# A relative-position bias table in DRAM: written by one copy from DRAM one layer earlier, not from eight partitions inside the layer that reads it

## The chip, the core and the metric

The program runs on one NeuronCore of one Trainium2 chip. Its engines have separate instruction streams: PE (TensorE, matrix products), DVE (VectorE), ACT (ScalarE), POOL (GpSimd) and SP (SyncE, which here only issues DMAs). DMAs are issued by SP or by ACT, each on a queue of its own; the profile calls SP's q1 and ACT's q10. The metric is the device time of one execution in microseconds (us), lower is better.

## The reference

The reference runs two transformer-like blocks on 512 tokens of 1024 features, in float32. The second block has an even layer (retention and gated recurrence), an odd layer, and after each of them cross-attention with a memory and a convolved feed-forward. The change concerns the odd layer's mixer, an attention with eight heads of 128. To each score it adds a bias that depends on the distance of query and key alone. Three dilated branches are merged; in the kernel they are one causal attention, in which a key counts as often as branches hold its distance:

```
logits = q.k * hd**-0.5 + rel_bias[bucket(distance)] (by head)
weight of a key = number of branches that hold its distance (none: left out)
o = softmax(logits, counted by branch) @ v, by head; x = x + o @ w_out
```

So all that a head needs as a bias is one row of 640 numbers, one for each distance. For a tile of 128 queries by up to 512 keys, each query reads this row one place further on than the query before it.

## The kernel before

Activations stay on the chip, feature-major, as eight tiles of 128 features by 512 tokens. Float32 products are made of three products each: activations and weights are split in a high and a low part (`whi`, `wlo` for weights), and `proj` (lines 487, 490 and 491) multiplies high by high, low by high and high by low. Weights come in groups of 1 MB. `fetch` (L461) issues the load on SP's queue into `wraw`, which has two buffers; `wload` cuts it into pieces of 128x512, ACT casts a piece to `whi` (L474) and POOL makes `wlo` (L383). `whi` and `wlo` have four buffers each, and a piece feeds twelve products on PE.

The ten layer parts run in the order m0, f0, m1, f1, ev, xa0, g0, od, xa1, g1. Here g0 is the feed-forward part before the odd mixer od. In g0, `up_pair` makes two of 22 tiles: projections to `psb` and `ps`, DVE's `pad` and `cv`, ACT's L600 and L603, and the split of the result to `mid` (ACT's cast at L496).

In od, `_odd` first makes the bias. Table `tb` (33x640, constant) and `relb` (33x8) come by SP's queue, two products on PE give `ps` (8x640), DVE copies it to `fb` on 8 partitions, one partition to a head, and a DMA on SP's queue writes each head's row 128 times to DRAM, at a step of 641 numbers, as `biasscr`. Read back at a step of 640, row q of the table is thus shifted by q. `head` reads 256 KB of it as `bias` (three buffers) with one DMA for each head, and DVE adds it to the scores where it takes them out of PSUM (L1570). For eight heads, `qkv` of the next head is projected beside `head` of the present one; `ps` of the scores (L1568) has two buffers.

The program is written in Tile: it gives dependences, and a scheduler with a timing model puts each engine's instructions in order. An engine runs its stream in that order; a DMA that waits holds up what stands behind it in its issuer's stream. All DMAs take one of eight completion semaphores in turn, and a DMA waits until the one before it on its semaphore has landed.

Of the kernel before, what the change touches and what calls it, by code (L numbers as in the profile page):

```python
# [11 lines left out]
F32 = mybir.dt.float32  # L12
# [8 lines left out]
P = 128  # L21
# [3 lines left out]
EPS = 1e-6  # L25
# [5 lines left out]
# ---------------------------------------------------------------- host layout  # L31
def _perm_attn():
    """Columns of a pair of 64-wide heads: first rope halves of both, then second halves."""
    idx = []
    for half in range(2):
        for h in range(2):
            for ax in range(2):
                idx += [h * 64 + ax * 32 + half * 16 + f for f in range(16)]
    return np.array(idx)
# [5 lines left out]
def _pack_cols(w, kc, cg):  # L45
    """[L, kc*128, G*cg] -> [L, G, 128, kc*cg]: one contiguous run per partition."""
    w = np.asarray(w)
    L, K, N = w.shape
    g = N // cg
    a = w.reshape(L, kc, P, g, cg).transpose(0, 3, 2, 1, 4)  # L50
    return np.ascontiguousarray(a).reshape(L, g, P, kc * cg)


def _cols(v):
    """[..., n*128] -> [128, n] of the flattened vector."""
    return np.asarray(v).reshape(-1, P).T
# [5 lines left out]
def _vec_layout(inputs=None):  # L62
    """All per-feature vectors as columns of one [128, n] array; fills VEC with the places."""
# [12 lines left out]
    for l in range(DEPTH):  # L76
        add(f"nm{l}", 8, lambda: _cols(g("norm_mix_g")[l]))
        add(f"nf{l}", 8, lambda: _cols(g("norm_ffn_g")[l]))
        # conv taps: column = tile*5 + tap
# [3 lines left out]
        # (dir, pair) columns, the head of the pair by partition half  # L83
# [26 lines left out]
def _const_layout():  # L110
    """Constants of the shapes alone, [128, n] float32."""
# [57 lines left out]
# the heads of the even mixer in turn: 0 for a recurrent one, 1 for a retention one  # L169
EV_HEADS = ((1, 0), (0, 0), (1, 1), (0, 1), (1, 2), (0, 2), (0, 3), (1, 3))  # L170
RET_CDECAY = [float((1.0 - 2.0 ** (-5.0 - h)) ** P) for h in range(4)]
# columns of the retention table
# [4 lines left out]
def _hg_masks():  # L177
    """Causal pairs (key, query) of a block of 8; for blocks of 16 and 32, keys of the lower halves
    with the queries of the upper halves, which stand side by side."""
# [11 lines left out]
def _dsa_tables():  # L191
    """Rows 0-31: one-hot of the bucket of a distance; row 32: log of the number of branches that
    hold the distance, -1e30 where none does. Column m stands for distance 512 - m."""
# [12 lines left out]
def host_arrays(inputs):  # L206
# [15 lines left out]
    # z, and the rows of its product's projection: heads 0 2, 1 3, 4 6, 5 7 side by side  # L222
# [14 lines left out]
    # tiles of 128: the forget gates; by head in turn, its columns; outputs by head in turn  # L237
# [4 lines left out]
    # by head: q, k, v columns side by side  # L242
# [9 lines left out]
# steps of the fillers of the first block's mixer to one of what they stand beside: the work inside the  # L252
# chunks, the inverse, the scan, the attention; the parts of the first gates beside the first
# two; the second gates left for the ends of the scan and of the attention
# [5 lines left out]
# ---------------------------------------------------------------- the program  # L260
class Norm:
    """RMS norm of the feature-major residual: chunks x*g split in two float32r parts; the
    reciprocal root of each token, on all partitions, is applied where products leave PSUM."""
# [8 lines left out]
    def chunk(self, m):  # L272
# [12 lines left out]
        # the sums of the last chunk apart, the others' are done by then  # L285
# [7 lines left out]
        if self.n == 8:  # L293
            k.tok_sums(self.sums[:, 1], sq)
            k.tt(self.sums[:, 0], self.sums[:, 0], self.sums[:, 1], ALU.add)
            # the roots by token, their squares
# [9 lines left out]
class Prog:  # L306
    def __init__(self, ctx, tc, A, out, first):
# [19 lines left out]
        # the first weights amid the residual  # L327
# [12 lines left out]
    def banks(self, *bufs):  # L340
        """The PSUM banks besides those of the projections, in up to three rings."""
# [10 lines left out]
    @contextmanager  # L352
    def phase(self, name):
        """The pool of a layer part: temporaries by role."""
        with self.tc.tile_pool(name=f"ph_{name}", bufs=1) as self.ph:
            yield self.ph

    def gs(self, name, bufs=2, shape=(P, S), dt=F32):
        """A temporary of a role: its buffers go round in program order."""
# [25 lines left out]
    def rsqrt(self, out, in_, scale, eps):  # L385
        """out = (in_ * scale + eps) ** -0.5: a first guess from the exponent, Newton steps to
        float32's accuracy."""
# [12 lines left out]
    def issue_behind(self, ins, before):  # L400
        """Issue order on an engine, no wait."""
# [3 lines left out]
    # ---- head norms: reciprocal roots by tokens, then spread over the partitions  # L405
    def tok_sums(self, out, sq, view=None, nt=4, psum=None):
        """Of a feature-major tile: the sums by token over all features, or those that view(by token)
        ends with, [128 tok, nt, ...]."""
# [9 lines left out]
    def rs_cols(self, groups, view, ncol, scale, eps, nt=4, psum=None, r=None):  # L418
        """For each group, a feature-major tile of squares: the sums by token over the features that
        view(by token) ends with, [128 tok, nt, ncol] ** -0.5; with the norm r, of products  # L420
        that its root has not been applied to yet, times that root."""
# [20 lines left out]
    def spread(self, rc, wide=None, nt=4, psum=None):  # L442
        """PSUM [128, nt*128]: per token its column of rc on all partitions; wide(e, rc) lays the
        columns out over the partitions where there are several."""
# [13 lines left out]
    # ---- weights  # L458
# [5 lines left out]
    def wload(self, src, kc, cg, rows=False):  # L464
        """One group of weight columns: a list of 128 columns each, as pieces (first row tile, its
        two float32r parts [128, 4, 128]); or the pieces [128, 2, 256] of all its columns."""
# [13 lines left out]
    def proj(self, ps, w, acts, n=S, behind=None):  # L480
        """ps := the product; behind: the instruction to issue it behind."""
# [11 lines left out]
    def split(self, dst, src, eng="vector"):  # L493
        """dst [128, 2, n] float32r := the two parts of src (SBUF or, on the vector engine, PSUM)."""
# [14 lines left out]
    def silu2(self, x, out, t):  # L509
        """out = 2 silu(x), t a scratch tile"""  # L510
# [4 lines left out]
    def to_tok(self, src, o, n=4, eng="scalar", scale=None, ps=None):  # L515
        """o [128 tok, n, 128] of a feature-major tile."""
# [12 lines left out]
    # ---- out projection onto the residual  # L529
# [27 lines left out]
    # ---- feed-forward layers  # L557
    def ffn(self, l, second, nm, nxt):
# [3 lines left out]
        with self.phase("ffn") as fp, self.banks(2, 2):  # L562
# [62 lines left out]
            for mp in range(5):  # L625
                up_pair(mp)
            down(0)
# [7 lines left out]
    # ---- first block: attention beside the delta net  # L635
# [4 lines left out]
    def _mix(self, l, nm, nxt, mp):  # L640
# [4 lines left out]
        # by direction, pair, chunk: the keys with their decays; by head of the pair, what makes the outputs,  # L645
        # the queries with their decays in the head's rows, the products in the other's
# [5 lines left out]
        # inverses by direction and pair of chunks  # L652
# [32 lines left out]
        # -- q, k, v of the delta net: projection, convolution, silu  # L685
# [12 lines left out]
        kq = []                             # by pair: keys, queries  # L698
# [10 lines left out]
        # -- l2 norms of q and k  # L709
# [4 lines left out]
        def l2(pairs):  # L714
# [6 lines left out]
            # x comes doubled; the queries times dk ** -0.5  # L721
# [6 lines left out]
        # -- beta and decay, by (head of the pair, token of the chunk)  # L728
# [26 lines left out]
        # log(1 + e) = log(u) + (e - (u - 1)) / u for the rounded u = 1 + e  # L755
# [37 lines left out]
        def by_chunk(dst, src, ps, scale):  # L793
            """dst (head of the pair, token of the chunk), by chunks, of a feature-major pair"""
# [7 lines left out]
        # -- v, by token  # L802
# [11 lines left out]
        # -- inside the chunks: decays, products of keys and queries  # L814
# [49 lines left out]
        # -- the fillers: attention, its projection and gate  # L864
# [6 lines left out]
        def gained(w, gname):  # L871
            """The products of a tile of two heads times the gain, their squares; the root of the norm
            is still to be applied."""
# [13 lines left out]
        def qkv():  # L887
            """Keys of a group in both halves of the rows of each rope half, in two parts; values in
            two parts."""
# [19 lines left out]
        def queries(g):  # L909
            """By head, the second part where the other head of its tile stood; the scores take the  # L910
            roots, by token."""
# [97 lines left out]
        # -- inverse of the unit triangles, one to a partition  # L1009
        def solve(sp):  # L1010
# [5 lines left out]
            # the halves of the diagonal first  # L1016
# [9 lines left out]
            # for their joining: the first half's transpose in the free corner, forwards; both halves  # L1026
            # transposed, the second itself in the corner, backwards
# [16 lines left out]
        def merge(*gens):  # L1044
            """In turn."""
# [9 lines left out]
        class Side:  # L1055
            """A generator whose steps are spread over those of others."""
# [52 lines left out]
        # -- the scan over the chunks, both directions  # L1109
# [4 lines left out]
        # what is wanted of two chunks at a time: columns by head of the pair, the other's rows 0  # L1114
# [18 lines left out]
        # pairs of chunks in turn of the directions  # L1133
        pair = lambda u: (u % 2, u // 2 if u % 2 == 0 else 3 - u // 2)

        def load(u):
            """Keys and queries of two chunks."""
# [8 lines left out]
        def join(u):  # L1146
            """The inverses of two chunks from their halves."""
# [11 lines left out]
            # the chunks side by side in the array  # L1159
# [18 lines left out]
        def scan_step(n):  # L1178
# [8 lines left out]
            def times(w, x):  # L1187
                """By pair the block's columns of each head times x."""
# [6 lines left out]
            # by head its state in its rows, the new values in the other's  # L1195
# [60 lines left out]
        # -- norm of the outputs, gated by z, feature-major again  # L1256
# [12 lines left out]
        # half of the root: z comes as 2 silu(z)  # L1269
# [4 lines left out]
        # by tiles of two heads of the same place in their pairs  # L1274
# [28 lines left out]
    # ---- even mixer: retention heads and gated recurrent heads  # L1303
# [4 lines left out]
    def _even(self, nm, nxt, ep):  # L1308
# [10 lines left out]
        # lower bounds of the forget gates: softmax over the rows, its first row  # L1319
# [12 lines left out]
        # f = lb + (1 - lb) (1 + tanh(x / 2)) / 2 = fa tanh(x / 2) + fb  # L1332
# [449 lines left out]
```

## Time and profile before

| | |
|---|---|
| median of 3 runs | 3497.29 us (3495.54 to 3500.16) |
| profiled execution, span from its first to its last instruction | 3496.1 us |
| PE busy | 3232.1 us, 92% |
| DVE, ACT, POOL busy | 58%, 42%, 52% |
| DMA traffic | 342.51 MB, on average 98 GB/s |

The page gives the profiled execution by its span alone; the median of the runs is 1.2 us above that. PE is busy nearly throughout, so that a stretch in which it stands still is to be looked for. An engine's idle time is put down to what ended it: "PE ps L1568 <- DVE pr L1570" is PE at the products of line 1568, waiting for a DVE instruction of line 1570 that writes `pr`. Times within the execution count from the span's start.

### The profile page before, as it was taken

The numbers are of one execution on the slowest core, as the hardware profiler recorded it, in microseconds if no ns is written. First come the engines' busy times: TensorE is split into PE (matmuls) and PEld (weight loads), VectorE is DVE, ScalarE is ACT, GpSimd is POOL, SyncE is SP. The second block draws the span as 40 slices with busy tenths as digits, with TensorE's granted clock in tenths as the row PEclk, the third lists the DMA queues.
The fourth block names the chain that finished last, engine by engine and source line by source line (L and its number), as shares of the span: only waits on it lengthen the run. The fifth ranks groups of instructions, "written<-read, shape, count | busy, mean of one in ns | idle before, by whom it ended". The sixth has DMA issues, their size and how long they took to land. (4 is left out here: it accounts for less than half of the span.)

```text
span 3496.1 us, 46894 instructions
## 1 busy us (share of the span) xinstructions
PE 3232.1 (92%) x17342; PEld 2661.3 (76%) x17342; DVE 2028.2 (58%) x3571; ACT 1483.6 (42%) x2766; POOL 1806.7 (52%) x1493
## 2 busy tenths in 40 slices
PE   8878899999978889999999888999997799899999
PEld 6666778888766677888878777888885687878887
DVE  8988556463698855555466676552323586663222
ACT  4536434343553553434353335443433355544332
POOL 4653365444565335554456556465554235556554
PEclk9999999999999999999999999999998899999999
DMA  4532532222353244222222113222223312222222
GB/s 142 161 88 61 132 122 86 100 94 94 122 159 102 72 113 128 87 97 97 94 101 86 59 62 109 73 97 97 97 91 91 84 61 103 91 90 89 95 98 93
DMA packets 135844, 342.51 MB, mean 98 GB/s; under 512 B 43039, under 2 KB 80287, under 8 KB 106944
## 3 DMA queue, kind: packets, MB, share of 16 engines
q1 hardware_dynamic: 135328, 338.75, 30.5%
q8 instruction: 138, 2.26, 0.3%
q14 instruction: 90, 0.74, 0.1%
q10 hardware_dynamic: 288, 0.76, 0.1%
HBM read 309.53 MB, written 29.95 MB: 97 GB/s over the span
## 5 line engine op out<-in xcount | busy, mean ns | idle before, releaser
L383 POOL TENSOR_TENSOR wlo<-wraw,whi 128x512 fp32r<-128x512 f32 (+2 forms) x1044 | 1370.2, 1316 | 1449.5 <-ACT whi L474 1402.0
L474 ACT CAST whi<-wraw 128x512 fp32r<-128x512 f32 (+2 forms) x1044 | 631.4, 608 | 1134.3 <-PE psb L490 838.4
L487 PE MATMUL psb<-act,whi 128*128 128x512 f32 x1888 | 760.6, 403 | 60.3 <-DVE x L383 19.8
L491 PE MATMUL psb<-act,wlo 128*128 128x512 f32 x1888 | 752.7, 399 | 3.5 <-POOL wlo L383 3.4
L490 PE MATMUL psb<-act,whi 128*128 128x512 f32 x1888 | 755.0, 400 | 0.6 <-DVE act L277 0.6
L487 PEld LDWEIGHTS psb<-act,whi 128*128 128x128 f32 x1888 | 364.5, 193 | 140.8 <-issue 43.0
L491 PEld LDWEIGHTS psb<-act,wlo 128*128 128x128 f32 x1888 | 363.4, 192 | 81.6 <-POOL wlo L383 5.8
L490 PEld LDWEIGHTS psb<-act,whi 128*128 128x128 f32 x1888 | 364.3, 193 | 74.2 <-DVE act L277 1.9
L383 DVE TENSOR_TENSOR x<-psb,x 128x512 f32<-128x512 f32 x168 | 115.2, 689 | 378.1 <-PE psb L491 377.5
L487 PE MATMUL ps<-act,whi 128*128 128x512 f32 (+1 forms) x720 | 281.6, 391 | 3.4 <-ACT rB L303 3.4
L491 PE MATMUL ps<-act,wlo 128*128 128x512 f32 (+1 forms) x720 | 281.0, 390 | 0.0
L490 PE MATMUL ps<-act,whi 128*128 128x512 f32 (+1 forms) x720 | 281.0, 390 | 0.0
L487 PE MATMUL psb<-mid,whi 128*128 128x512 f32 x704 | 277.0, 394 | 1.0 <-DVE x L383 1.0
L491 PE MATMUL psb<-mid,wlo 128*128 128x512 f32 x704 | 276.2, 392 | 0.0
L490 PE MATMUL psb<-mid,whi 128*128 128x512 f32 x704 | 274.1, 389 | 0.0
L487 PEld LDWEIGHTS ps<-act,whi 128*128 128x128 f32 (+1 forms) x720 | 134.1, 186 | 33.8 <-ACT rB L303 4.6
L491 PEld LDWEIGHTS ps<-act,wlo 128*128 128x128 f32 (+1 forms) x720 | 134.1, 186 | 29.8 <-issue 0.8
L490 PEld LDWEIGHTS ps<-act,whi 128*128 128x128 f32 (+1 forms) x720 | 134.2, 186 | 29.3 <-issue 0.5
L491 PEld LDWEIGHTS psb<-mid,wlo 128*128 128x128 f32 x704 | 132.3, 188 | 30.3
L487 PEld LDWEIGHTS psb<-mid,whi 128*128 128x128 f32 x704 | 132.6, 188 | 29.4 <-DVE x L383 1.5
L490 PEld LDWEIGHTS psb<-mid,whi 128*128 128x128 f32 x704 | 132.3, 188 | 29.1
L383 DVE TENSOR_TENSOR cv<-ps,cv 128x512 f32<-128x512 f32 (+1 forms) x60 | 41.5, 692 | 175.8 <-PE ps L491 106.1
(437 smaller groups left out, 5712.8 us busy)
## 6 DMA issues: line engine op xcount, KB each, us to landing
wraw<-in_wup SPq DMA_DIRECT2D x44, 1024.0 KB, 4.8
wraw<-in_fup SPq DMA_DIRECT2D x44, 1024.0 KB, 4.8
wraw<-in_win SPq DMA_DIRECT2D x38, 1024.0 KB, 5.0
wraw<-in_wdn SPq DMA_DIRECT2D x16, 1024.0 KB, 4.8
wraw<-in_evin SPq DMA_DIRECT2D x16, 1024.0 KB, 4.8
wraw<-in_xakv SPq DMA_DIRECT2D x16, 1024.0 KB, 4.8
wraw<-in_fdn SPq DMA_DIRECT2D x16, 1024.0 KB, 4.9
wraw<-in_odin SPq DMA_DIRECT2D x12, 1024.0 KB, 4.8
```

What stands on the lines that cost most here:

```text
L383: getattr(self.nc, eng).tensor_tensor(out, a, b, op)
L474: nc.scalar.copy(hi, part)
L487: mm = nc.tensor.matmul(ps, hi[:, i], acts[k][:, 0, :n], start=k == 0, stop=False)
L490: nc.tensor.matmul(ps, hi[:, i], acts[k][:, 1, :n], start=False, stop=False)
L491: nc.tensor.matmul(ps, lo[:, i], acts[k][:, 0, :n], start=False, stop=k == kc - 1)
```

## The change

The making of the table moves out of `_odd` into a function `bias_rows`, which g0's `ffn` calls after its third `up_pair`, in the layer before the odd mixer. Its four DMAs are issued by ACT on ACT's queue. `fb` is first written to DRAM as `biasrow` (8 rows of 2560 bytes), and then one DMA from DRAM to DRAM copies these 128 times to `biasscr`. In this DMA the 128 copies are the outermost dimension, and the heads the next; before, the heads were the outermost. `tb`, `relb` and `fb` now lie in g0's pool. `_odd` only reads the finished table. The diff's other lines take out comments and docstrings, so that line numbers shift (L1560 to L1568, L1568 to L1576, L1570 to L1578).

```diff
@@ ffn @@
             for mp in range(5):
                 up_pair(mp)
+                if mp == 2 and l == 0 and second:
+                    self.bias_rows(fp)
             down(0)
...
+    def bias_rows(self, op):
+        nc = self.nc
+        tb, rb = op.tile([33, 640], F32, name="tb"), op.tile([33, 8], F32, name="relb")
+        nc.scalar.dma_start(out=tb, in_=self.A["dsat"])
+        nc.scalar.dma_start(out=rb, in_=self.A["relb"])
+        fb = op.tile([8, 640], F32, name="fb")
+        for a, b in ((0, 512), (512, 640)):
+            ps = self.pss()
+            nc.tensor.matmul(ps[:8, :b - a], rb, tb[:, a:b], start=True, stop=True)
+            nc.vector.tensor_copy(fb[:, a:b], ps[:8, :b - a])
+        row = self.dr.tile([8, 640], F32, name="biasrow")
+        nc.scalar.dma_start(out=row, in_=fb)
+        self.biasscr = self.dr.tile([8, P * 641], F32, name="biasscr")
+        nc.scalar.dma_start(out=self.biasscr.rearrange("h (q m) -> q h m", m=641)[:, :, :640],
+                            in_=row.unsqueeze(0).broadcast_to((P, 8, 640)))
...
     def _odd(self, nm, nxt, op):
         nc, gs = self.nc, self.gs
         win = self.A["odin"][0]
-        tb = op.tile([33, 640], F32, name="tb", tag="pT", bufs=2)
-        nc.sync.dma_start(out=tb, in_=self.A["dsat"])
-        rb = op.tile([33, 8], F32, name="relb")
-        nc.sync.dma_start(out=rb, in_=self.A["relb"])
-        scr = self.dr.tile([8, P * 641], F32, name="biasscr")
-        fb = op.tile([8, 640], F32, name="fb", tag="pT", bufs=2)
...
-        nc.sync.dma_start(out=scr.rearrange("h (q m) -> h q m", m=641)[:, :, :640], in_=fb.unsqueeze(1).broadcast_to((8, P, 640)))
+        scr = self.biasscr
```

Three places show how the scheduler's order moves. The first is SP's queue at the beginning of the odd mixer; `wraw<-in_odin` are the mixer's weight loads. Before:

```order
L461 DMA wraw<-in_odin 128x2048 x2
L1511 DMA tb<-in_dsat 33x640
L1513 DMA relb<-in_relb 33x8
L461 DMA wraw<-in_odin 128x2048 x2
L1521 DMA biasscr<-fb 1024x1x640
L461 DMA wraw<-in_odin 128x2048
L1560 DMA bias<-biasscr 128x512 x3
L461 DMA wraw<-in_odin 128x2048
```

The same place of the changed kernel:

```order
L461 DMA wraw<-in_odin 128x2048 x2
L1568 DMA bias<-biasscr 128x512 x3
L461 DMA wraw<-in_odin 128x2048 x4
L1568 DMA bias<-biasscr 128x512
L461 DMA wraw<-in_odin 128x2048
```

The write of the table is gone from this queue, and the first three heads' reads of it stand two weight loads after the mixer's first, where `tb` and `relb` stood.

The second place is ACT in g0, after the sixth tile's `mid`; DMAHW4_49 and the like are the semaphores that a row waits for. Changed kernel only (before, the rows are the same without the two DMAs):

```order
L496 CAST mid<-cv 128x512 [waits DVE_49]
L1516 DMA biasrow<-fb 8x640 [waits DMAHW4_49,DVE_49]
L474 CAST whi<-wraw 128x512 [waits DMAHW2_49,PE_49,Pool_49]
L1518 DMA biasscr<-biasrow 128x8x640 [waits DMAHW4_49]
L474 CAST whi<-wraw 128x512 [waits PE_49,Pool_49]
L600 ACTIVATE cv<-pad_20213,vect 128x512 [waits DVE_49]
```

The copy waits on ACT until `biasrow` has landed in DRAM, and a weight cast and the seventh tile's L600 stand behind it. The loads of `tb` and `relb` stand on ACT some forty rows earlier. The copy holds semaphore DMAHW5. The first DMA after it on SP's queue that waits for DMAHW5 is the ninth weight load from the one that is issued beside the copy.

The third place is PE at the mixer's first head, with the projections of `psb` left out. `sq` are the sums for the norms of query and key, `rc` the spreading of the key's roots, `x` the transposes of the values, `qk` the scores. Before:

```order
L1519 MATMUL ps_22872<-tb,relb 8x512
L1519 MATMUL ps_22875<-tb,relb 8x128
...
L412 MATMUL ps_22929<-cstt,sq 128x128 x4
L412 MATMUL ps_22982<-cstt,sq 128x128 x4
...
L455 MATMUL ps_23003<-cstt,rc 128x128 x4
L1553 MATMUL ps_23056<-cstt,x 128x128 x4
L1568 MATMUL ps_23234<-qk 128x128
```

The same place of the changed kernel:

```order
L412 MATMUL ps_22931<-cstt,sq 128x128 x4
L412 MATMUL ps_22984<-cstt,sq 128x128 x4
...
L455 MATMUL ps_23005<-cstt,rc 128x128 x4
L1561 MATMUL ps_23058<-cstt,x 128x128 x4
L1576 MATMUL ps_23236<-qk 128x128
```

The two table products are gone from here, and the `sq` products stand in their place, 22 projection products earlier. Between `sq` and `rc` there were 12 projection products, and now there are 34.

## Rows read from the trace of the kernel before

**Rows 1.** The page: busy time of PE, with its share.
```profile
PE 3232.1 (92%) x17342; PEld 2661.3 (76%) x17342; DVE 2028.2 (58%) x3571; ACT 1483.6 (42%) x2766; POOL 1806.7 (52%) x1493
```
**Rows 2.** Waits, 2650 to 2950 us: waiter <- releaser: us, times, longest.
```profile
PE ps L1568 <- DVE pr L1570: 44.0, 1, 44.0
...
PE ps L1568 <- ACT qk L496: 1.2, 1, 1.2
```
**Rows 3.** Waits of SP's DMA queue, the same stretch.
```profile
SPq L1560 <- DMA biasscr<-fb: 35.6, 1, 35.6
```
**Rows 4.** Timeline of SP in the odd mixer: start us, duration us, instruction.
```profile
2652.91 0.37 SPq L1511 DMA_DIRECT2D tb<-in_dsat  x1
...
2675.73 0.80 SPq L1521 DMA_DIRECT2D biasscr<-fb  x1
2679.38 15.48 SPq L461 DMA_DIRECT2D wraw<-in_odin  x1
2730.51 1.28 SPq L1560 DMA_DIRECT2D bias<-biasscr  x3
```
**Rows 5.** Weight loads issued 2640 to 2760 us, line 461 on SP's queue.
```profile
DMA to landing us min/median/max: 4.7/4.8/53.6
```
**Rows 6.** Windows: length, busy us (count) of PE, PEld, DVE, ACT, POOL, PEclk, DMA, GB/s.
```profile
2400.00:2500.00 100.00, 100.00 (x440) 82.52 (x440) 23.98 (x33) 33.01 (x52) 53.95 (x43) 1.00 0.27 95
...
2685.00:2690.00 5.00, 2.56 (x14) 2.08 (x14) 3.42 (x6) 2.06 (x4) 0.69 (x1) 0.87 0.47 50
2705.00:2725.00 20.00, 0.00 (x0) 0.00 (x0) 0.00 (x0) 0.00 (x0) 0.00 (x0) 0.50 0.47 49
2740.00:2800.00 60.00, 60.00 (x316) 50.81 (x315) 45.33 (x153) 28.24 (x73) 20.65 (x16) 1.00 0.24 84
```
**Rows 7.** Timeline of PE at the first head: idle before it in brackets.
```profile
2673.77 1.24 PE L1519 MATMUL ps<-tb,relb 33*8 33x512 f32 x4
...
2680.06 1.03 PE L412 MATMUL ps<-cstt,sq 128*128 128x128 f32 x8
...
2685.93 0.62 PE L455 MATMUL ps<-cstt,rc 128*128 128x128 f32 x4 [2.08 <-DVE rc L383]
...
2688.99 1.23 PE L1568 MATMUL ps<-qk 128*128 128x128 f32 x4 [0.31 <-DVE qk L498]
2734.17 1.33 PE L1568 MATMUL ps<-qk 128*128 128x384 f32 x3 [43.96 <-DVE pr L1570]
...
2736.01 0.78 PE L487 MATMUL psb<-act,whi 128*128 128x512 f32 x1
...
2739.95 0.40 PE L487 MATMUL psb<-act,whi 128*128 128x512 f32 x1
```
**Rows 8.** Timeline of DVE at the first head, from the bias to the weights.
```profile
2733.77 0.35 DVE L1570 SCALAR_TENSOR_TENSOR pr<-ps,rc,bias 128x128 f32<-128x128 f32 x1 [44.17 <-DMA bias<-biasscr]
...
2737.46 0.34 DVE L1575 TENSOR_SCALAR pr<-pr,mx 128x256 f32<-128x256 f32 x1
```
**Rows 9.** Timeline of ACT in g0, weight casts after the sixth tile's `mid`.
```profile
2359.94 0.62 ACT L474 CAST whi<-wraw 128x512 fp32r<-128x512 f32 x1 [0.80 <-PE psb L490]
2362.67 0.62 ACT L474 CAST whi<-wraw 128x512 fp32r<-128x512 f32 x1 [2.11 <-PE psb L490]
...
2371.05 0.62 ACT L474 CAST whi<-wraw 128x512 fp32r<-128x512 f32 x1 [2.09 <-PE ps L490]
```
**Rows 10.** Timeline of SP in g0, two of its weight loads.
```profile
2359.26 0.33 SPq L461 DMA_DIRECT2D wraw<-in_fup  x1
...
2446.73 0.33 SPq L461 DMA_DIRECT2D wraw<-in_fup  x1
```
**Rows 11.** DMA issues of the whole execution: count, KB each, median us to landing.
```profile
wraw<-in_fup SPq DMA_DIRECT2D x44, 1024.0 KB, 4.8
...
scrG<-gct SPq DMA_DIRECT2D x2, 32.0 KB, 2.0
```
**Rows 12.** A DMA of ACT's queue in the first 25 us, beside SP's loads.
```profile
cstt<-in_cst ACTq DMA_DIRECT2D x1, 384.0 KB, 5.0
```

More of the change, by code (lines that the diff above doesn't have):

```diff
@@ L1508, in _odd @@
         win = self.A["odin"][0]
-        tb = op.tile([33, 640], F32, name="tb", tag="pT", bufs=2)
-        nc.sync.dma_start(out=tb, in_=self.A["dsat"])
-        rb = op.tile([33, 8], F32, name="relb")
-        nc.sync.dma_start(out=rb, in_=self.A["relb"])
-        scr = self.dr.tile([8, P * 641], F32, name="biasscr")
-        fb = op.tile([8, 640], F32, name="fb", tag="pT", bufs=2)
-        for a, b in ((0, 512), (512, 640)):
-            ps = self.pss()
-            nc.tensor.matmul(ps[:8, :b - a], rb, tb[:, a:b], start=True, stop=True)
-            nc.vector.tensor_copy(fb[:, a:b], ps[:8, :b - a])
-        nc.sync.dma_start(out=scr.rearrange("h (q m) -> h q m", m=641)[:, :, :640], in_=fb.unsqueeze(1).broadcast_to((8, P, 640)))
+        scr = self.biasscr
         def roots(ps, scale, eps):
```

## The prediction

> **What bounds the kernel now.** I read the page's busy times first, then the waits of the odd mixer, then the timelines around the longest one. PE is busy for 92% of the span [rows 1], so an edit is worth what it takes from PE's idle or slow time, and little else. In the odd mixer one wait is larger than all others: PE stands still for 44.0 us [rows 2]. Follow it back. PE waits at the first head's third score product, because both score buffers are full; DVE, which empties them, waits 44.17 us for `bias` [rows 8]; and SP cannot issue the reads of `bias` until 2730.51, since it waits for `biasscr<-fb` to land, 35.6 us of it after the last thing SP had to do before [rows 3, 4]. The write of the table was issued at 2675.73 [rows 4], so it took some 54 us. From 2740 to 2800 PE is busy without a gap, at full clock [rows 6]. The stall is therefore one hole, not a rate.
>
> **The stall.** In the changed kernel the table is in DRAM long before. The place in g0 is the one after the sixth tile; there ACT casts at 2359.94 and 2362.67 [rows 9], so the copy is issued at about 2361, and the reads stand on SP where `tb` stood, which went at 2652.91 [rows 4]. That leaves the copy 290 us. The term is -44.0 us; its bounds are 0 (the table is late all the same) and -44.0.
>
> **What stands before it.** PE waits 2.08 us for `rc`, the key's roots, at 2685.93 [rows 7]. The chain begins with the end of the `sq` products, at 2681.09, and takes 4.84 us. Before, 12 projection products stood in between, and one takes 100 / 440 = 0.227 us [rows 6], 2.7 us in all; now there are 34, which is 7.7 us. So the wait should go: -2.1 us, between 0 and -2.1. The waits of the scores for the two halves of the key, 1.2 us [rows 2] and 0.31 us [rows 7], have the same products around them, and I leave them as they are (bounds 0 and -1.5).
>
> **What is late next.** With the bias there, the third score product waits only until DVE has taken the first scores out, 0.35 us [rows 8], which can start while PE makes the second ones: +0.3 us, between 0 and +0.4. Then the softmax of the first two query tiles needs 2737.80 - 2733.77 = 4.0 us on DVE and ACT [rows 8]. PE has 24 projection products before it needs the result, as before, and these are 5.4 us at full clock. That covers it with little to spare: 0, up to +5 if the first head's chain is longer.
>
> **The clock.** The granted clock is 0.87 from 2685 to 2690 and 0.50, the 1.2 GHz level, while PE stands still; from 2740 it is 1.00, or 2.4 GHz [rows 6]. PE's work just beside the stall ran at the lower level. Nine projection products took 2739.95 - 2736.01 = 3.94 us [rows 7] where nine at full clock take 2.05, so 1.9 is lost; the 1.84 us from 2734.17 to 2736.01 and the 1.23 us at 2688.99 [rows 7] would each take half, which is 1.5 more. Without the stall there is nothing for the clock to fall after but waits of about 1 us: -3.4 us, between 0 and -3.4.
>
> **The table products.** They take 1.24 us of PE in the odd mixer [rows 7] and the same in g0, where PE is as full (100.00 us of 100 [rows 6]). 0, between -1.2 and +1.2.
>
> **ACT in g0.** It now issues four DMAs. Issues of this kind took 0.37 and 0.80 us on SP [rows 4], so this is about 2 us, and the copy waits for `biasrow` to land. The nearest small write, 32 KB, landed after 2.0 us [rows 11]. Behind it stand a weight cast and L600. ACT idles 0.80 and 2.11 us before the casts here, waiting for PE to free a buffer [rows 9], and PE has three pieces of twelve products in hand at such a moment, 3 x 2.7 = 8.2 us. I take 0; if the cover failed, +2.
>
> **The copy beside g0's weights.** This is the cost that moves rather than goes. While only the old write ran, DMA was busy 0.47 of 16 engines, at 49 GB/s [rows 6]. That is 7.5 engines at 6.5 GB/s each, or 0.39 us for a packet of 2560 bytes. The table has 8 x 128 = 1024 such packets. Spread over 16 engines, 64 each, they would take 25 us if a packet is no faster from DRAM; over 8, as before, 53 us. A weight load is 1 MB in 8 KB rows, 8 to an engine. The load issued at 2359.26 [rows 10] normally lands in 4.8 us [rows 11], and its first cast comes at 2371.05 [rows 9], 7.0 us later. After that cast is due, PE still has 8.2 us of pieces, less 0.62 for the cast and 1.3 for POOL: about 6 us. So a load may be 13 us late. If packets of the two queues alternate, it is 8 x 0.39 = 3.1 us late, which is hidden: 0. If it has to wait for the whole copy on 16 engines, it is 25 us late and PE stands for 12: the upper bound is +12. The row against me is the mixer's own load issued behind the old write: its issue alone took 15.48 us [rows 4], and it landed after 53.6 us instead of 4.8 [rows 5]. But that was one queue; where two queues had work, at the start, ACT's 384 KB landed in 5.0 us beside SP's loads [rows 12]. I take 0.
>
> The Trainium skill speaks against hoping for a free queue here: "DMA: Bandwidth & Descriptors", section "Issuing engines are not separate DMA queues", says that DMAs of all issuers run on the same 16 engines and interleave. By that rule the copy costs the weights their share, the 3.1 us above, and does not stop them; by the row of the 53.6 us it would stop them. The sum is -49.2 by the rule and -37 by the row.
>
> The same page, section "Why a DMA increments its semaphore by 16 and not by 1", says that a DMA runs on the largest number of engines up to 16 that divides the slowest dimension of both sides. By it the old write has 8 engines, with which the 7.5 agree, and the new copy 16, which no run here shows yet.
>
> **Sum.** -44.0 - 2.1 + 0.3 - 3.4 = -49.2 us. From the span, 3496.1, that is 3446.9. The median of the runs lies 1.2 above the span, so I forecast 3448 us. The case's own range is 3442 to 3454: the waits that I leave may go too (-1.5), the clock may not come back at once (+3.4), runs of before spread by -1.8 and +2.9.
>
> **Rivals.**
> - *The first head becomes the bound.* The stall gave DVE and ACT time to clear their work, and now the softmax chain of 4.0 us is open for the first two heads. For it: DVE is busy 45.33 of 60 us after the stall [rows 6]. Against: PE has no gap there at that load. It costs 4 to 8 us: 3454.
> - *The copy stops the weights.* As worked out, +12: 3460. The landing after 53.6 us [rows 5] speaks for it, the separate queues against.
> - *The change doesn't do what it says.* The reads of `bias` could still be late, if SP came to them late. They wait for PE and DVE to be done with g0's buffers, as `tb` did, which went 37 us before the scores need them. No gain: 3497.
> - *The copy is slow, and SP stops at its semaphore.* The ninth weight load after it, issued at 2446.73 before [rows 10], waits on the copy's semaphore, which leaves it 2446.73 - 2361 = 86 us, and 13 us more in hand. Copies that read the same 20 KB of DRAM 128 times are not in this trace. Beyond 99 us PE stands in g0, and from 99 + 49 = 148 us on the kernel is slower than before. If the copy ran on one engine, 1024 x 0.39 = 400 us, the time would be 3448 + 301 = 3749. Against it: even the old write, on eight partitions, took 54.
>
> **How the numbers follow.** The forecast gets 0.80, the first head 0.08, stopped weights 0.07, no effect 0.03, the slow copy 0.02. The first three are faster by more than 0.2% (7 us, about what a measurement of this kernel tells from no change): 0.95; same 0.03; slower 0.02. The range runs from 3440, the lowest sum less the spread of runs, to 3462, which takes in stopped weights.
>
> **What would show it.** Right: no wait of DVE for `bias`; PE without a hole near 2690 and the clock at 1.00 there; the copy landed 25 to 55 us after its issue; g0 as full as before. A wait of PE for `rc` of 2 us again takes the second term back. Weight loads in g0 that land after 20 us or more, with PE idle behind them, mean that the row of the 53.6 us was the better guide. The forecast is wrong if DVE still waits for `bias`, or if g0 grows by more than 5 us.

## The result, and the profile after

| | before | after |
|---|---|---|
| median of 4 runs each | 3497.8 us (3495.54 to 3500.16) | 3454.85 us (3445.89 to 3461.62) |
| ratio, with its 95% interval | | 0.9874 (0.9857 to 0.9891) |
| span of the profiled execution | 3496.1 us | 3444.1 us |

The change takes 43 us off the median, where 49 were forecast. The time lies 7 us above the forecast of 3448: within the whole range of 3440 to 3462, but 0.9 above the forecast case's own range of 3442 to 3454, and on the figure of the rival in which the first head becomes the bound. The median alone therefore doesn't tell the two apart; the stages below do. The page after, in the line that answers to [rows 1]:

```profile
PE 3227.7 (94%) x17342; PEld 2655.6 (77%) x17342; DVE 2030.8 (59%) x3571; ACT 1483.2 (43%) x2766; POOL 1806.1 (52%) x1493
```

PE has the same number of instructions and nearly the same busy time (3232.1 us before). What went is idle time.

**Where the time went.** The profiled spans differ by 52.0 us, and not all of that is the change. Three lines cut the execution into stages: the weight loads of the feed-forward (`in_fup`, first issued at the start of g0), of the odd mixer (`in_odin`) and of its output (`in_odout`). Each line gives the shortest, median and longest issue in ns, then the starts of the first and the last. Before:

```profile
L461 SPq DMA_DIRECT2D wraw<-in_fup x44: 327/328/328, 2275.0 to 3428.5; - x44
...
L461 SPq DMA_DIRECT2D wraw<-in_odin x12: 327/333/15483, 2637.7 to 2838.0; - x12
...
L461 SPq DMA_DIRECT2D wraw<-in_odout x8: 327/328/328, 2852.2 to 2914.1; - x8
```

The same lines after:

```profile
L461 SPq DMA_DIRECT2D wraw<-in_fup x44: 327/328/328, 2268.1 to 3376.4; - x44
...
L461 SPq DMA_DIRECT2D wraw<-in_odin x12: 327/328/333, 2632.4 to 2784.4; - x12
...
L461 SPq DMA_DIRECT2D wraw<-in_odout x8: 327/328/328, 2798.1 to 2860.3; - x8
```

Subtract first starts. Stage g0 took 2637.7 - 2275.0 = 362.7 us before and 364.3 after; stage od took 214.5 and 165.7. Together that is 577.2 and 530.0, so the change is worth -47.2 us in the two stages that it touches. Another -6.9 us lie ahead of g0, where it touches nothing, and +2.1 behind od. Two profiles of one and the same kernel (below) differ ahead of g0 by 13 us, so that part is spread, and this profile was a lucky one. The stages are the better gauge, and each experiment is read by them as well as by its time.

**The stall.** No wait of DVE for `bias` is left. SP's timeline in the odd mixer, as in [rows 4] (start, duration, instruction):

```profile
2647.60 1.28 SPq L1568 DMA_DIRECT2D bias<-biasscr  x3
2649.55 42.35 SPq L461 DMA_DIRECT2D wraw<-in_odin  x4
```

The three reads go at 2647.60, some 33 us before the scores need them; the write and the 15.48 us issue behind it are gone. (The second row is four issues in one, from the start of the first to the end of the last; none of the mixer's takes over 0.333 us.) PE's timeline at the first head, as in [rows 7]:

```profile
2668.40 1.04 PE L412 MATMUL ps<-cstt,sq 128*128 128x128 f32 x8
...
2676.99 0.60 PE L455 MATMUL ps<-cstt,rc 128*128 128x128 f32 x4
...
2679.28 0.49 PE L1576 MATMUL ps<-qk 128*128 128x128 f32 x2 [1.25 <-ACT qk L496]
2680.08 0.72 PE L1576 MATMUL ps<-qk 128*128 128x128 f32 x4 [0.31 <-DVE qk L498]
2681.00 1.33 PE L1576 MATMUL ps<-qk 128*128 128x384 f32 x3 [0.20 <-DVE pr L1578]
```

The third score product waits 0.20 us in place of 43.96. The wait for `rc` is gone, and the two for the halves of the key are as long as before. But the clock did not stay up. Windows, with columns as in [rows 6]:

```profile
2358.00:2364.00 6.00, 6.00 (x28) 4.99 (x27) 1.75 (x3) 2.59 (x4) 4.08 (x4) 1.00 1.04 212
2680.00:2681.00 1.00, 0.72 (x4) 0.52 (x4) 1.00 (x4) 0.28 (x1) 0.00 (x0) 0.96 0.00 0
2681.00:2682.00 1.00, 1.00 (x3) 1.00 (x4) 0.86 (x3) 0.98 (x3) 0.00 (x0) 0.50 0.00 0
2682.00:2684.00 2.00, 2.00 (x9) 1.71 (x8) 0.97 (x3) 1.99 (x5) 0.00 (x0) 0.50 0.00 0
2684.00:2685.00 1.00, 1.00 (x6) 0.79 (x5) 1.00 (x4) 0.21 (x3) 0.00 (x0) 0.83 0.00 0
...
2700.00:2800.00 100.00, 100.00 (x528) 84.78 (x527) 79.66 (x268) 52.41 (x140) 33.51 (x26) 1.00 0.23 77
```

PE had run without a break until it idled 1.25, 0.31 and 0.20 us between 2678 and 2681. Then the granted clock stands at 0.50, the 1.2 GHz level, for three microseconds in which PE is busy, and is back at 1.00 (2.4 GHz) by 2685. Summed over the four short rows in the middle, (1 - clock) times length is 0.04 + 0.50 + 1.00 + 0.17 = 1.7 us. From 2700 to 2800 PE has no gap. In the whole stage od it is idle for 1.76 us (165.70 long, 163.94 busy; the row stands at late_act_copy), and that is these three waits.

**The copy.** ACT's timeline in g0, beside [rows 9]:

```profile
2351.78 0.62 ACT L496 CAST mid<-cv 128x512 fp32r<-128x512 f32 x1 [0.65 <-DVE cv L383]
2352.56 0.28 ACTq L1516 DMA_DIRECT2D biasrow<-fb  x1
2354.61 0.62 ACT L474 CAST whi<-wraw 128x512 fp32r<-128x512 f32 x1 [2.21 <-PE psb L490]
2354.64 0.65 ACTq L1518 DMA_DIRECT2D biasscr<-biasrow  x1
2357.34 0.62 ACT L474 CAST whi<-wraw 128x512 fp32r<-128x512 f32 x1 [2.11 <-PE psb L490]
```

The casts around the copy still wait for PE, 2.21 and 2.11 us, so they are not late on ACT. Microseconds from issue to landing, in this order for the DMAs that write or read `biasscr` (the longest is the copy), for g0's weight loads between 2300 and 2460, and for the mixer's weight loads:

```profile
DMA to landing us min/median/max: 2.7/4.0/14.9
...
DMA to landing us min/median/max: 4.6/4.8/6.9
...
DMA to landing us min/median/max: 4.7/4.9/5.7
```

The copy landed after 14.9 us; the old write took some 54. One weight load in g0 was 2.1 us late. The mixer's loads no longer have one of 53.6 us [rows 5]. In the first window above, the busy share of the 16 DMA engines is 1.04 at 212 GB/s, and PE is busy in all 6.00 us. The one late load is the first behind the copy. It was issued 10.4 us after it, when 4.5 of the copy's 14.9 us were left:

```profile
2365.03 0.33 SPq L461 DMA_DIRECT2D wraw<-in_fup  x1
```

### The profile page after: what moved, and what is told of

Its sections match the earlier page's. It is cut to its first block, busy times and chain, and to the rows that moved or that the text cites. A ratio compares the mean times of both kernels' runs of the same rounds, so it can differ in the third digit from the quotient of the medians.

```text
span 3444.1 us, 46891 instructions
## 1 busy us (share of the span) xinstructions
PE 3227.7 (94%) x17342; PEld 2655.6 (77%) x17342; DVE 2030.8 (59%) x3571; ACT 1483.2 (43%) x2766; POOL 1806.1 (52%) x1493
## 5 line engine op out<-in xcount | busy, mean ns | idle before, releaser
L491 PEld LDWEIGHTS ps<-act,wlo 128*128 128x128 f32 (+1 forms) x720 | 133.9, 186 | 29.4
```

Source lines behind the costliest of these rows:

```text
L491: nc.tensor.matmul(ps, lo[:, i], acts[k][:, 0, :n], start=False, stop=k == kc - 1)
```

## The experiments

All edits are to the changed kernel. The change has three parts: the place (g0 and not od), the queue (ACT's and not SP's) and the form (a copy from DRAM and not a write from 8 partitions; "fan" below is the old form). The ratios are to the kernel before, run on the same chip; its medians there were 3499.3 us (13 runs, 3491.22 to 3506.31) in the first four experiments and 3500.28 (3496.7 to 3507.89) in the others.

| kernel | place, queue, form | median us | ratio (95% interval) | g0 | od | sum |
|---|---|---|---|---|---|---|
| before | od, SP, fan | | 1 | 362.7 | 214.5 | 577.2 |
| after | g0, ACT, copy | 3454.85 | 0.9874 (0.9857 to 0.9891) | 364.3 | 165.7 | 530.0 |
| after_again | g0, ACT, copy | 3453.54 | 0.9873 (0.9852 to 0.9894) | 364.3 | 165.7 | 530.0 |
| early_act_fan | g0, ACT, fan | 3462.25 | 0.9894 (0.9873 to 0.9914) | 372.1 | 164.8 | 536.9 |
| early_sp_fan | g0, SP, fan | 3488.26 | 0.9973 (0.9961 to 0.9984) | 395.7 | 165.4 | 561.1 |
| late_act_copy | od, ACT, copy | 3459.74 | 0.9895 (0.9871 to 0.9919) | 362.7 | 174.7 | 537.4 |
| early_sp_copy | g0, SP, copy | 3452.94 | 0.9864 (0.9848 to 0.9881) | 364.1 | 165.7 | 529.8 |
| early_act_copy_heads | g0, ACT, copy, heads outermost | 3452.51 | 0.9865 (0.985 to 0.988) | 364.3 | 165.7 | 530.0 |
| early_act_part128 | g0, ACT, from 128 partitions | 3464.64, one run | | 375.0 | 165.3 | 540.3 |
| late_act_fan | od, ACT, fan | 3498.93 | 0.9994 (0.9985 to 1.0003) | 362.7 | 214.4 | 577.1 |

**after_again: no edit, to see what repeats.**

> The changed kernel once more, to separate its gain from its spread (3445.89 to 3461.62 in four runs). Between the mixer's first weight load and its output projection's first weight load, before took 214.5 us and the changed kernel 165.7; if the gain is the table's lateness alone, this stretch is again within 2 us of 166, g0 is within 2 us of 364, and what spreads lies in parts that the change doesn't touch. If the spread comes from the change (the copy beside g0's weights), it shows in g0 or in the mixer.

The ratio came again, and the stages came again to the tenth of a microsecond. What did not repeat is the time at which g0 begins, 2281.5 us and not 2268.1:

```profile
L461 SPq DMA_DIRECT2D wraw<-in_fup x44: 327/328/328, 2281.5 to 3387.3; - x44
...
L461 SPq DMA_DIRECT2D wraw<-in_odin x12: 327/328/333, 2645.8 to 2797.8; - x12
...
L461 SPq DMA_DIRECT2D wraw<-in_odout x8: 327/328/328, 2811.5 to 2873.7; - x8
```

So what differs between these two profiles lies outside the change, 13.4 us of it ahead of g0. What in those parts varies stays open.

**early_act_fan: the old form, at the new place and on the new queue.**

```diff
-        row = self.dr.tile([8, 640], F32, name="biasrow")
-        nc.scalar.dma_start(out=row, in_=fb)
...
-        nc.scalar.dma_start(out=self.biasscr.rearrange("h (q m) -> q h m", m=641)[:, :, :640],
-                            in_=row.unsqueeze(0).broadcast_to((P, 8, 640)))
+        nc.scalar.dma_start(out=self.biasscr.rearrange("h (q m) -> h q m", m=641)[:, :, :640],
+                            in_=fb.unsqueeze(1).broadcast_to((8, P, 640)))
```

> The table is made in g0 and on ACT's queue as in the changed kernel, but by the old DMA from 8 partitions: 1024 packets of 0.39 us on 8 engines, some 53 us. Theory 1 (only the table's lateness counted; packets of two queues alternate): a weight load beside it lands at most some 4 us late, PE stays full in g0, and the time is the changed kernel's, 3455 within its spread. Theory 2 (the copy from DRAM is needed, since the old write holds up weights on whatever queue): one load in g0 lands after 50 us, PE stands 36 to 40 us, 3490 to 3495.

Neither theory holds: one load is late, and not by 4 us or by 50. The stages are 6.9 us longer than after: 7.8 more in g0, 0.9 less in od. A window of four microseconds while the write ran:

```profile
2364.00:2368.00 4.00, 4.00 (x20) 3.30 (x19) 1.54 (x2) 1.89 (x3) 2.12 (x2) 1.00 0.45 49
```

This is the rate of [rows 6] again, 7.2 engines at 6.8 GB/s each, or 0.38 us for a packet. One weight load of g0 landed after 21.3 us, 16.5 late, and the one behind it after 14.0. What waited, as waiter and releaser, us, times, longest:

```profile
ACT whi L474 <- DMA wraw<-in_fup: 10.9, 1, 10.9
PE ps L487 <- ACT whi L474: 5.8, 1, 5.8
```

A load that is 16.5 us late costs PE 5.8, so the cover is 10.7 us. The prediction had 13. Its upper bound, weights that the copy stops, is a real mechanism, which the slow form sets off. The late load's issue, and three windows behind it:

```profile
2370.71 0.33 SPq L461 DMA_DIRECT2D wraw<-in_fup  x1
...
2371.50:2375.00 3.50, 3.50 (x17) 2.88 (x16) 2.30 (x3) 1.96 (x4) 1.76 (x2) 1.00 0.89 202
2375.00:2382.00 7.00, 7.00 (x32) 5.82 (x31) 2.89 (x4) 3.09 (x5) 4.67 (x4) 1.00 0.46 50
...
2385.30:2394.50 9.20, 3.37 (x12) 2.47 (x11) 0.84 (x2) 1.86 (x3) 1.70 (x2) 0.74 0.52 165
```

The first window carries 152 GB/s beyond the write's 50 for 3.5 us, which is 0.53 MB or half of the load. In the next 7 us nothing moves but the write. The rest comes late, beside part of the next load. So the packets of the two queues do not alternate one by one: half of the load comes at once, and half stands in one piece. Why it stands is not shown. In the last window the clock is at 0.74. PE's busy time in g0 is 364.94 us where it was 362.96 after, so that the lower clock cost 2.0 of the 7.8 us beside the wait of 5.8.

Od shows something of the clock, too. PE waited 1.25, 0.31 and 0.19 us at the first head, as after; but here the clock stayed at 1.00:

```profile
2694.50:2698.00 3.50, 3.50 (x18) 3.03 (x19) 2.31 (x7) 3.06 (x7) 0.00 (x0) 1.00 0.00 0
```

So these waits do not by themselves bring the clock down; what else decides it is open.

**early_sp_fan: the place alone.**

```diff
-        nc.scalar.dma_start(out=tb, in_=self.A["dsat"])
-        nc.scalar.dma_start(out=rb, in_=self.A["relb"])
+        nc.sync.dma_start(out=tb, in_=self.A["dsat"])
+        nc.sync.dma_start(out=rb, in_=self.A["relb"])
...
-        nc.scalar.dma_start(out=row, in_=fb)
...
+        nc.sync.dma_start(out=self.biasscr.rearrange("h (q m) -> h q m", m=641)[:, :, :640],
+                            in_=fb.unsqueeze(1).broadcast_to((8, P, 640)))
```

> Only the place is changed: the table is made in g0, by the old DMA from 8 partitions on SP's queue. Theory 1 with one queue: the load issued behind the write lands after 45 to 54 us as in the odd mixer before; 13 us of that are covered, so PE stands 30 to 40 us in g0 and the time is 3485 to 3495: the stall has moved, not gone. Rival (loads in one queue go beside the write, and the 53.6 us of before were an accident): no stall, 3455.

As the first theory said, the stall moved: the odd mixer gains its 49.1 us, and g0 gives 33.0 of them back. SP's timeline in g0, the write and the weight loads behind it:

```profile
2361.18 0.81 SPq L1516 DMA_DIRECT2D biasscr<-fb  x1
2373.28 10.17 SPq L461 DMA_DIRECT2D wraw<-in_fup  x1
2383.93 4.17 SPq L461 DMA_DIRECT2D wraw<-in_fdn  x1
```

The waits that end on PE:

```profile
ACT whi L474 <- DMA wraw<-in_fup: 34.4, 1, 34.4
PE ps L487 <- ACT whi L474: 29.4, 1, 29.4
```

The load behind the write on the same queue landed after 44.9 us, 40.1 late, and PE stood for 29.4: the cover is 10.7 us again. This is the row of the 53.6 us [rows 5] at its new place. On ACT's queue the same write delays a load by 16.5.

The Trainium skill ("DMA: Bandwidth & Descriptors", section "Issuing engines are not separate DMA queues") says that issuing from several engines saves only the time of the issue. For the fan in g0 the runs do not agree: the queue alone is worth 561.1 - 536.9 = 24.2 us, and the measurement decides. For the copy, below, the stages agree, and so they do for the fan in od, where nobody waits for the load (late_act_fan).

**late_act_copy: queue and form without the place.**

```diff
-                if mp == 2 and l == 0 and second:
-                    self.bias_rows(fp)
...
-        nc.scalar.dma_start(out=tb, in_=self.A["dsat"])
-        nc.scalar.dma_start(out=rb, in_=self.A["relb"])
+        nc.sync.dma_start(out=tb, in_=self.A["dsat"])
+        nc.sync.dma_start(out=rb, in_=self.A["relb"])
...
+        self.bias_rows(op)
         scr = self.biasscr
```

> The place is undone: the table is made in the odd mixer, with its loads on SP's queue as before, but written by biasrow and the copy from DRAM on ACT's queue. Theory 1: fb is ready about 15 us before the scores need the bias; 2 us for biasrow, 15 for the copy, 4 for the read make 21, so PE stands 6 to 9 us and the time is 7 to 11 us over the changed kernel's, 3462 to 3466. Theory 2 (the place is what counts, the way of writing little): PE stands over 30 us, 3485 or more.

Form and queue together bring 39.8 of the 47.2 us; that the queue adds nothing here is seen with the fan only (late_act_fan). The copy was issued at 2676.90 and landed after 15.6 us; the reads went at 2692.47, and PE never waited for them, since the order had projections in the meantime; 6 to 9 us of waiting had been expected. Od is 9.0 us longer than after. PE's waits of over a microsecond in od, the last of them at a second `rc`:

```profile
2685.44 0.62 PE L455 MATMUL ps<-cstt,rc 128*128 128x128 f32 x4 [2.07 <-DVE rc L383]
...
2687.70 2.03 PE L1575 MATMUL ps<-qk 128*128 128x128 f32 x6 [1.19 <-ACT qk L496]
...
2710.85 0.78 PE L455 MATMUL ps<-cstt,rc 128*128 128x128 f32 x4 [1.97 <-DVE rc L383]
```

The whole stage od of this kernel in one window, and two short ones in it:

```profile
2637.20:2811.90 174.70, 169.00 (x832) 139.79 (x831) 119.18 (x375) 81.44 (x193) 66.04 (x52) 0.97 0.30 101
...
2690.00:2695.00 5.00, 5.00 (x16) 4.09 (x16) 0.01 (x1) 1.51 (x2) 0.00 (x0) 0.59 0.42 144
...
2710.00:2720.00 10.00, 9.15 (x44) 8.05 (x45) 7.30 (x23) 6.03 (x17) 3.43 (x3) 0.83 0.06 8
```

The same stage before and after:

```profile
2637.70:2852.20 214.50, 166.96 (x831) 139.03 (x830) 116.83 (x372) 82.10 (x192) 65.72 (x52) 0.88 0.31 82
...
2632.40:2798.10 165.70, 163.94 (x828) 137.49 (x827) 116.13 (x374) 82.25 (x196) 65.79 (x52) 0.99 0.26 90
```

PE is idle for 174.70 - 169.00 = 5.7 us against 1.8 after, which is 3.9 of the 9.0, about the two waits for `rc`. It is busy 5.1 longer: 1.24 are the table products, and the other 3.8 go with the lower clock, of which the short windows show where. With the place undone the first head's wait for `rc` is back, at 2.07 us: the second term goes with the table products' place.

This run also shows what the copy does to a load right behind it. The load issued at 2678.89, 2.0 us after the copy, landed after 11.7 us, 6.9 late.

**early_sp_copy: only the queue undone.**

```diff
-        nc.scalar.dma_start(out=row, in_=fb)
+        nc.sync.dma_start(out=row, in_=fb)
...
-        nc.scalar.dma_start(out=self.biasscr.rearrange("h (q m) -> q h m", m=641)[:, :, :640],
+        nc.sync.dma_start(out=self.biasscr.rearrange("h (q m) -> q h m", m=641)[:, :, :640],
```

(The loads of `tb` and `relb` move too, as in early_sp_fan.)

> As the changed kernel, with its four table DMAs on SP's queue: place and form are kept, the queue is undone. The copy takes 14 to 15 us; a load issued behind it in one queue lands that much late. From the runs with the old write in g0, weights have 10.7 us of cover (a load 16.5 us late cost PE 5.8, one 40.1 late cost 29.4). Theory 1: the load lands after 17 to 20 us, PE stands 2 to 5 us, and g0 takes 366 to 370 us where the changed kernel takes 364.3. Rival (a second queue is worth nothing, the traffic alone counts): landing under 8 us, no wait of PE, 364.

The stages take 529.8 us, as after, so the queue is worth nothing here once the copy comes from DRAM. Neither expectation is met in full: the time is the rival's, the landing (below) lies between the two. SP's timeline shows why the next load was not very late:

```profile
2368.14 0.61 SPq L1518 DMA_DIRECT2D biasscr<-biasrow  x1
2375.67 0.34 SPq L461 DMA_DIRECT2D wraw<-in_fup  x1
```

It was issued 7.5 us after the copy, half of whose 14.7 us were over. It landed after 9.3 us, 4.5 late, inside the cover of 10.7. A load that stands right behind the copy on one queue is in none of the runs.

**early_act_copy_heads: only the order of the copy's dimensions undone.**

```diff
-        nc.scalar.dma_start(out=self.biasscr.rearrange("h (q m) -> q h m", m=641)[:, :, :640],
-                            in_=row.unsqueeze(0).broadcast_to((P, 8, 640)))
+        nc.scalar.dma_start(out=self.biasscr.rearrange("h (q m) -> h q m", m=641)[:, :, :640],
+                            in_=row.unsqueeze(1).broadcast_to((8, P, 640)))
```

> As the changed kernel, but the copy has the eight heads outermost again, so that it may use 8 engines. Packets from DRAM took 0.13 us at the median beside 0.38 for those from 8 partitions. If the source is what makes a packet slow, the copy lands after 16 to 25 us on 8 engines (0.13 to 0.2 us x 128), weights are hardly late, and the time is the changed kernel's. If eight engines alone made the old write slow, it lands after about 50 us and the weights are late as with the old write on ACT's queue (g0 370 to 373 us).

```profile
2368.00:2372.00 4.00, 4.00 (x20) 3.30 (x19) 0.74 (x1) 1.77 (x3) 2.71 (x3) 1.00 0.52 194
```

This window, while the copy ran, has DMA at 0.52 of 16 engines, about 8, and 194 GB/s. So 8 engines carry nearly as much as 16 did at 212, and the stages are the same, though the load that was issued 10.4 us after the copy landed after 9.0 us here and after 6.9 with 16. The Trainium skill's rule that the slowest dimension sets the number of engines ("DMA: Bandwidth & Descriptors", section "Why a DMA increments its semaphore by 16 and not by 1") agrees with these shares: 0.45 and 0.52 with 8 outermost, 1.04 with 128. As the expectation's first case has it, the number of engines is not what made the copy fast.

**early_act_part128: from 128 partitions, without the copy.** The table is made 8 times as 128 equal rows, by 16 products, and each head's rows leave in one DMA of 128 packets.

```diff
+        for h in range(8):
+            fb = op.tile([P, 640], F32, name="fb", tag="fb", bufs=2)
...
+                nc.tensor.matmul(ps[:, :b - a], rb[:, h:h + 1].broadcast_to((33, P)), tb[:, a:b], start=True, stop=True)
...
+            nc.scalar.dma_start(out=self.biasscr[h].rearrange("(q m) -> q m", m=641)[:, :640], in_=fb)
```

> The price of a packet by its source: the table's rows are made on all 128 partitions by 16 products with relb's column repeated, and written to the same places of DRAM by eight DMAs of 128 packets of 2560 bytes, from 128 partitions instead of 8. If a packet is slow because its partition is read again and again, these take 0.10 to 0.15 us each and a DMA of 128 lands in 3 to 4 us; if writes of 2560 bytes from SBUF at a step of 2564 are slow by themselves, they take 0.37 to 0.39 and a DMA lands after 5 us. PE spends about 9 us more in g0; the time is not the point here.

```profile
2372.00:2374.00 2.00, 2.00 (x10) 1.66 (x9) 1.38 (x2) 0.55 (x1) 0.82 (x1) 1.00 0.38 149
```

In this window 6.1 engines move 149 GB/s, 24.5 each: 0.10 us for a packet of the same 2560 bytes into the same places in DRAM. The first case of the expectation holds: neither the step in DRAM nor a source on the chip made the old write slow. What is left is the source: 8 partitions, each read 128 times over. Whether it is the repeated reading or that there are only 8 partitions, no run tells, since both change together here; a write of 8 partitions that are read once each would. G0 grew by 10.7 us, and so did PE's busy time in it (373.66 us, and 362.96 after), most of it by the further products: those of one head take 1.34 us.

**late_act_fan: the queue alone.** The edit of late_act_copy puts the place back and that of early_act_fan the form, so that against the kernel before only the queue of the write differs:

```diff
-                if mp == 2 and l == 0 and second:
-                    self.bias_rows(fp)
...
-        nc.scalar.dma_start(out=self.biasscr.rearrange("h (q m) -> q h m", m=641)[:, :, :640],
-                            in_=row.unsqueeze(0).broadcast_to((P, 8, 640)))
+        nc.scalar.dma_start(out=self.biasscr.rearrange("h (q m) -> h q m", m=641)[:, :, :640],
+                            in_=fb.unsqueeze(1).broadcast_to((8, P, 640)))
...
+        self.bias_rows(op)
         scr = self.biasscr
```

> Only the queue is changed: the table is made in the odd mixer by the old write from 8 partitions, but on ACT's queue. Theory 1 (the table's lateness alone): it still lands some 54 us after fb, so DVE and PE wait about as long as before, and the odd mixer takes 205 to 214.5 us as before (changed kernel 165.7), time 3490 to 3500. Rival (part of the stall was SP's queue: the weight load stuck 53.6 us behind the write): the mixer is 5 us or more under 205.

```profile
DVE pr L1575 <- DMA bias<-biasscr: 44.1, 1, 44.1
PE ps L1573 <- DVE pr L1575: 43.9, 1, 43.9
```

The stall is untouched, as the first theory said. The mixer's load beside the write landed after 20.3 us and not 53.6, but nobody was waiting for it.

## Why the prediction was right, and by how much it was off

- *The stall, -44.0.* Right: PE's wait fell from 43.96 to 0.20 us. The place brings this by itself (od 165.4 in early_sp_fan), and so does, by the table's earlier landing, the form on ACT's queue (no wait of PE for `bias` in late_act_copy).
- *The wait for `rc`, -2.1.* Right, and shown by its return in late_act_copy.
- *Key halves kept, third score product +0.3, softmax hidden.* Right: 1.25 and 0.31, 0.20, and no gap on PE from 2700 to 2800. The rival in which the first head becomes the bound did not come, though the median lies on its figure.
- *The clock, -3.4.* This term was mis-sized. It said that without the stall there are only waits of about 1 us for the clock to fall after. It fell, to 0.50, behind 1.25, 0.31 and 0.20 us, and took back 1.7 us, half of the term. PE's busy time in od agrees: it fell from 166.96 to 163.94 us, of which 1.24 are the table products and 1.8 are left for the clock. A row of before had the sign: at 0.87 from 2685 to 2690 [rows 6], the clock had been low for 0.13 x 5 / 0.5 = 1.3 us there, so that it fell near 2688.7, while the stall began only at 2734.17 - 43.96 = 2690.2 [rows 7].
- *Table products.* 0 net was forecast. They left od (1.24), and g0 grew by 1.6, so 0.4 are unexplained. Sum by stages: -49.2 + 1.7 + 0.4 = -47.1, against -47.2 measured.
- *ACT in g0, 0.* Right; the casts still wait for PE.
- *The copy beside the weights, 0.* The term was right, but its working was not. The price of 0.39 us a packet, from the old write, does not hold from DRAM: 14.9 us and not 25 to 55. Alternation of packets does not hold either (with the fan a load came 16.5 us late and not 3.1), and the cover is 10.7 us and not 13. The first error helps and the other two hurt: with the fan on ACT's queue the same place costs 7.8 us in g0 (early_act_fan). Some of the 0 is luck of timing: the next load was issued when 10.4 of the copy's 14.9 us were over. But even the load issued 2.0 us after the copy in late_act_copy was 6.9 us late, less than the cover found in g0.
- *The slow copy and SP's semaphore.* Not met: the copy landed after 14.9 us, and the load that waits on its semaphore had 86.
- *From the sum to the time.* -47.2 on the median of before would be 3450.6. The 4 us up to the measured 3454.85 are within the spread of 16 us of those runs; the two profiles of this kernel differ outside the two stages only, and after_again gave 3453.54.

None of the versions beats the changed kernel beyond that spread: early_sp_copy and early_act_copy_heads have its stages to 0.2 us.

## What to carry to other kernels

When a DMA's landing holds up a head of work, ask separately when it starts, how fast it runs and what it shares a queue with, and price each: here the form, with the new queue, was worth 39.8 us, the place alone 16.1, and the queue alone nothing. A slow DMA that is moved out of one wait takes its slowness along, and the weight loads behind it pay. With the fast copy the place was worth 537.4 - 530.0 = 7.4 us more and the queue nothing; with the slow write in g0 the queue was worth 24.2. Where runs spread by more than an effect, cut the execution at instructions on either side of the change and compare the stages.

## What was not expected of the hardware

- The write of 2560-byte packets from 8 partitions, each read 128 times, took 0.38 us a packet on an engine (early_act_fan); from 128 partitions it was 0.10 (early_act_part128), and from a 20 KB source in DRAM, read 128 times as well, about 0.11 (8.3 engines at 194 GB/s, early_act_copy_heads).
- A copy from DRAM to DRAM ran near 200 GB/s on 8 engines and on 16 (194 and 212; the latter window holds the copy alone, if the load issued at 2352.51 landed in the usual 4.8 us; the next was issued at 2365.03).
- Of a weight load on SP's queue beside the slow write on ACT's, half came at once, and then for 7 us nothing moved but the write's 50 GB/s (early_act_fan).
- Behind waits of PE of 1.25, 0.31 and 0.20 us, the granted clock stood at 0.50 for three busy microseconds; behind 1.25, 0.31 and 0.19 us in early_act_fan it stayed at 1.00.
